# Delta-rule stage: the low parts of the weight chunks move from GpSimd to VectorE

## The chip, the cores and the metric

The kernel runs on one core of a Trainium2 chip. Its time is the device time of that core in microseconds, the median of several executions. The engines are TensorE (PE; PEld is its weight load), VectorE (DVE), ScalarE (ACT), GpSimd (POOL) and SyncE (SP, which issues most of the transfers). The trace comes from one profiled execution.

## The reference, cut to what matters

Two layers work on a sequence of 256 rows and 2048 columns, the first also on a context of 256 rows. The first layer, with the delta rule (a linear recurrence over chunks of 64 rows, 16 heads, both directions), is the one in question:

```python
def _gdn_chunk_scan(q, k, v, g, beta, s0):
    ...
    m = jnp.where(strict, jnp.einsum('bhnid,bhnjd->bhnij', kb, k) * decay, 0.0)
    t_inv = lax.linalg.triangular_solve(eye + m, ..., lower=True, unit_diagonal=True)
    w = jnp.einsum('bhnij,bhnjd->bhnid', t_inv, kb * jnp.exp(gc)[..., None])
    u = jnp.einsum('bhnij,bhnjd->bhnid', t_inv, vb)
    a_intra = jnp.where(tril, jnp.einsum('bhnid,bhnjd->bhnij', q, k) * decay, 0.0)
    def step(S, xs):
        v_new = u_i - w_i @ S
        o = qg_i @ S + a_i @ v_new
        S = S * gl_i[..., None, None] + jnp.swapaxes(kg_i, -1, -2) @ v_new
        return S, o
...
qkv, z_a, ab, b_g, c_g, h_b, z_b = split(h @ w_in)      # projections
y_b = b_g * conv(c_g * h_b, w_conv_b) * silu(z_b)
y   = concat([rmsnorm(o, head_norm) * silu(z_a), y_b]) @ w_out
```

## The kernel before, in words

Every weight passes through `wchunk` (L194 to L214). A chunk of 128 x 1024 floats is loaded by SP into a tile `raw`; ACT rounds it to the format that PE multiplies fastest (`H`, L201); a low part `L` = raw - H is taken either on POOL (L206) or on DVE (L208). The projections then multiply three times per weight tile: H with the high part of the activations, H with their low part, L with their high part (`proj`, L229; `projT`, L238 to L240). There are four buffers each for `raw`, `H` and `L`. Which engine takes the low part is decided by a counter: each chunk adds `LP[stage]`, and when the counter reaches one, POOL takes it and one is subtracted. The stages are 0 (keys and values), 1 (the delta rule), 2 (the first output projection) and 3 (the second layer). Stage 1 has 220 chunks: 32 of wq and 32 of wza, 128 of wbb, and 28 of the output projection.

In stage 1 four groups of four heads are worked off one after the other; I call each a pass. A pass projects its queries (wq) and gate (wza), loads its keys and values from DRAM by POOL's queue (L687), and then runs, in the program's names:

- Gram matmuls `G` and `Q` (L737, L741) and the decay `E` (L746, L748) on PE, exponentials `Es` on ACT, the products `U` and `aT` on DVE (L756, L758);
- a triangular solve of 32 x 32 blocks on DVE: 30 rounds of a product (L778) and an addition (L780) on `LB`, each depending on the one before, with transposes and copies around it, the last ones into `UT` (L797);
- the inverse of the 128 x 128 blocks from these: `PT`, `XT`, `X`, `P` on PE (L806 to L844) with copies between;
- the recurrence, four steps in two directions: `z` (L880), `zk` and `zs` on ACT (L884, L887), `Sp` (L891) and the state `St` on DVE (L896), `kS` (L860), `r` on DVE (L863), `QS` (L868), `az` (L902); at the end the norm, `on` (L916) and the transposes `oT` (L919).

Then come the pass's shares of the projection wbb (3, 4, 5 and 4 blocks of eight chunks) with a short convolution (L930 to L941). Beside all this, `ada_step` loads 256 KB pieces of the modulation weights and accumulates them on DVE (L276).

The order of each engine's instructions is not that of the code: a list scheduler with its own estimate of times puts them in an order, fixed when the kernel is built, with priority for the pass's delta rule (`HP`). So projection chunks of the next pass stand between the solve and the recurrence of this one. Buffers set limits: PSUM has two tiles `pj` for projections and four `g` for everything else in the pass, given out in the code's order; the keys' tile exists once.

Of the kernel before, what the change touches and what calls it, by code (L numbers as in the profile page):

```python
# [29 lines left out]
HP = 1  # L30
FINK = 2
RATE = (2.5, 0.6, 1.2, 0.4)
LP = (0.5, 0.5, 0.4, 0.2)
CHUNKS = (1, 2, 4, 4, 5)
RADII = (1, 2, 4, 8)

# [85 lines left out]
def body(ctx: ExitStack, tc: tile.TileContext, T, dbg=None):  # L122
# [71 lines left out]
    def wchunk(src, nk, rp=None, hp=None, lp=None, sz=1024, HL=None):  # L194
# [7 lines left out]
        L = HL[1] if HL else (lp or wlp).tile([P, sz], F32R, name="L", tag="L")  # L202
        tick[3] += LP[tick[2]]
        if tick[3] >= 1.0:
# [987 lines left out]
```

## Time and profile before

| what | value |
|---|---|
| time, median of 3 runs (lowest to highest) | 2283.49 us (2281.34 to 2284.37) |
| the profiled execution's own time, its span | 2281.2 us, 2279.4 us |
| PE busy | 2102.5 us, 92% of the span |
| DVE busy | 1511.8 us, 66% |
| ACT busy | 992.0 us, 44% |
| POOL busy | 547.9 us, 24% |
| low parts on POOL (L206), on DVE (L208) | 205 at 2483 ns, 349 at 1285 ns in the mean |
| mean granted TensorE clock | 0.968 |

The shares are means over stages with different limits. Stage 1, from the first pass's G to the last pass's oT, lasts from 550 to 1453 us; what bounds it has to be read from that stretch and from its parts. A matmul's duration in the trace is longer than its distance to the next one, since matmuls are pipelined.

### The profile page before, as it was taken

Reading aid. Unit: us, or ns where it says so; the run is one execution under the profiler, and the core shown is the slowest. Engines: PE = TensorE matmul, PEld = TensorE weight load, DVE = VectorE, ACT = ScalarE, POOL = GpSimd, SP = SyncE. Lnnn points to the kernel's source line nnn. Section 1 sums busy time; section 2 is a strip of 40 time slices with the busy share of each in tenths; the row PEclk is TensorE's granted clock in tenths of the full one; section 3 lists DMA queues with packets and bytes.
Section 4 is the critical chain, followed back from the end, with each engine's and each line's share of the span. In section 5 each row is a group of like instructions: output and inputs, shape, how many; then the busy total and the mean of one; then the engine's idle time right before and its main releaser. Section 6 shows DMA issues by size and latency. Waiting matters only on the chain. (4 is left out here: it accounts for less than half of the span.)

```text
span 2279.4 us, 42114 instructions
## 1 busy us (share of the span) xinstructions
PE 2102.5 (92%) x17034; PEld 1951.4 (86%) x17034; DVE 1511.8 (66%) x2500; ACT 992.0 (44%) x1726; POOL 547.9 (24%) x258
## 2 busy tenths in 40 slices
PE   6998999899989988998899879898999999999998
PEld 4888989898979987998899868686789999999886
DVE  4336997658965896599658964666667676555445
ACT  4332354225544635553545354334444444444443
POOL 0112112123322332323232323232112111111221
PEclk9999999999989999999899989999999999999999
DMA  8776546668435663566356645686767656666664
GB/s 324 278 258 209 153 146 201 192 188 275 141 108 169 213 219 122 170 204 214 120 163 214 205 141 175 200 289 193 251 203 215 180 185 199 188 193 216 192 191 137
DMA packets 151267, 446.41 MB, mean 196 GB/s; under 512 B 16512, under 2 KB 23456, under 8 KB 150048
## 3 DMA queue, kind: packets, MB, share of 16 engines
q1 hardware_dynamic: 145936, 425.37, 58.7%
q0 software_dynamic: 5136, 18.35, 2.6%
q8 instruction: 133, 2.18, 0.4%
q14 instruction: 62, 0.51, 0.1%
HBM read 423.19 MB, written 20.46 MB: 195 GB/s over the span
## 5 line engine op out<-in xcount | busy, mean ns | idle before, releaser
L206 POOL TENSOR_TENSOR L<-raw,H 128x1024 fp32r<-128x1024 f32 (+1 forms) x205 | 508.7, 2483 | 1557.9 <-ACT H L201 1500.2
L201 ACT CAST H<-raw 128x1024 fp32r<-128x1024 f32 (+1 forms) x554 | 571.9, 1039 | 698.7 <-PE pj L229 302.3
L208 DVE TENSOR_TENSOR L<-raw,H 128x1024 fp32r<-128x1024 f32 (+1 forms) x349 | 447.8, 1285 | 311.2 <-ACT H L201 310.1
L229 PE MATMUL pj<-hxH,L 128*128 128x256 f32 x1856 | 537.7, 290 | 43.9 <-DVE L L208 43.7
L229 PE MATMUL pj<-hxH,H 128*128 128x256 f32 x1856 | 536.1, 289 | 4.8 <-DVE kacc L482 4.8
L229 PE MATMUL pj<-hxL,H 128*128 128x256 f32 x1856 | 535.0, 288 | 0.0
L229 PEld LDWEIGHTS pj<-hxH,L 128*128 128x128 f32 x1856 | 360.2, 194 | 51.6 <-DVE L L208 48.1
L229 PEld LDWEIGHTS pj<-hxH,H 128*128 128x128 f32 x1856 | 360.2, 194 | 6.9 <-DVE kacc L482 5.0
L229 PEld LDWEIGHTS pj<-hxL,H 128*128 128x128 f32 x1856 | 360.3, 194 | 1.4 <-issue 0.4
L276 DVE SCALAR_TENSOR_TENSOR acc<-araw,cs,acc 128x512 f32<-128x512 f32 x240 | 244.9, 1020 | 134.3 <-DMA araw<-in_ada 84.0
L229 PE MATMUL pj<-h1H,H 128*128 128x256 f32 x1024 | 290.6, 284 | 0.8 <-DVE yo L1052 0.8
L229 PE MATMUL pj<-h1H,L 128*128 128x256 f32 x1024 | 289.8, 283 | 0.0
L229 PE MATMUL pj<-h1L,H 128*128 128x256 f32 x1024 | 289.8, 283 | 0.0
L229 PEld LDWEIGHTS pj<-h1H,H 128*128 128x128 f32 x1024 | 196.5, 192 | 1.1 <-PE adc L286 0.8
L229 PEld LDWEIGHTS pj<-h1L,H 128*128 128x128 f32 x1024 | 196.5, 192 | 0.0
L229 PEld LDWEIGHTS pj<-h1H,L 128*128 128x128 f32 x1024 | 196.5, 192 | 0.0
L229 PE MATMUL pj<-hcH,H 128*128 128x256 f32 x320 | 92.0, 287 | 0.0
L229 PE MATMUL pj<-hcH,L 128*128 128x256 f32 x320 | 91.6, 286 | 0.0
L229 PE MATMUL pj<-hcL,H 128*128 128x256 f32 x320 | 91.5, 286 | 0.0
L238 PE MATMUL pj<-H,y1H 128*128 128x512 f32 x192 | 76.0, 396 | 0.0
L240 PE MATMUL pj<-H,y1L 128*128 128x512 f32 x192 | 75.9, 396 | 0.0
L239 PE MATMUL pj<-L,y1H 128*128 128x512 f32 x192 | 75.9, 395 | 0.0
(433 smaller groups left out, 3852.3 us busy)
## 6 DMA issues: line engine op xcount, KB each, us to landing
raw<-in_wbb SPq DMA_DIRECT2D x128, 512.0 KB, 4.1
raw<-in_wout SPq DMA_DIRECT2D x128, 512.0 KB, 4.5
araw<-in_ada SPq DMA_DIRECT2D x192, 256.0 KB, 3.4
raw<-in_ada SPq DMA_DIRECT2D x64, 512.0 KB, 6.4
raw<-in_wpz SPq DMA_DIRECT2D x64, 512.0 KB, 4.1
raw<-in_wuz SPq DMA_DIRECT2D x64, 512.0 KB, 3.9
raw<-in_wkv SPq DMA_DIRECT2D x40, 512.0 KB, 4.7
araw<-in_ada0g SPq DMA_DIRECT2D x64, 256.0 KB, 3.6
```

The source lines that it names most:

```text
L201: S.copy(H, raw)
L206: G.tensor_tensor(L, raw, H, ALU.subtract)
L208: V.tensor_tensor(L, raw, H, ALU.subtract)
L229: PE.matmul(o[:, e * 256:(e + 1) * 256] if m > 1 else o, w, a[t][:, k, :], start=st and i == 0 and e == 0, stop=sp and i == 2, skip_group_ ...
L238: PE.matmul(o, xH[:, t], H[:, kk, :], start=st, stop=False, skip_group_check=True)
L239: PE.matmul(o, xH[:, t], L[:, kk, :], start=False, stop=False, skip_group_check=True)
L240: PE.matmul(o, xL[:, t], H[:, kk, :], start=False, stop=sp, skip_group_check=True)
L276: V.scalar_tensor_tensor(aacc[u // KT], raw, cs[:, k, 0:1], aacc[u // KT], ALU.mult, ALU.add)
```

## The change

One number of the table `LP` changes, that of stage 1: no chunk there reaches the threshold, so `wchunk` takes its low part on DVE. The other stages keep their shares.

```diff
 RATE = (2.5, 0.6, 1.2, 0.4)
-LP = (0.5, 0.5, 0.4, 0.2)
+LP = (0.5, 0.0, 0.4, 0.2)
```

The scheduler makes a new order from it. On POOL, from the loads of the first pass's keys and values (`KTt`, `Kt`, `Vn`) to the load of the first layer's result (`yld`), only the loads are left:

```order
-L206 TENSOR_TENSOR L<-raw,H 128x1024 x19
+L206 TENSOR_TENSOR L<-raw,H 128x1024 x18
 L687 DMA KTt<-ktd 128x4x512
 L687 DMA Kt<-kkd 128x4x512
 L687 DMA Vn<-vvd 128x4x512
-L206 TENSOR_TENSOR L<-raw,H 128x1024 x26
 L687 DMA Kt<-kkd 128x4x512
-L206 TENSOR_TENSOR L<-raw,H 128x1024
```

110 low parts leave POOL in all. On DVE, in the middle of the second pass's solve (`ltmp` and `LB` are its product and its sum), there stood before:

```order
L778 TENSOR_TENSOR ltmp<-LB 128x234
L208 TENSOR_TENSOR L<-raw,H 128x1024
L276 SCALAR_TENSOR_TENSOR acc<-araw,cs,acc 128x512
L780 TENSOR_TENSOR LB<-LB,ltmp 128x18x13
L778 TENSOR_TENSOR ltmp<-LB 128x238
L931 TENSOR_TENSOR cg<-cg,pj 128x256
L276 SCALAR_TENSOR_TENSOR acc<-araw,cs,acc 128x512
L780 TENSOR_TENSOR LB<-LB,ltmp 128x17x14
L350 SCALAR_TENSOR_TENSOR cbt<-cg,cols,cbt 128x4x63
L778 TENSOR_TENSOR ltmp<-LB 128x240
L351 SCALAR_TENSOR_TENSOR cbt<-cg,cols,cbt 128x4x63
L208 TENSOR_TENSOR L<-raw,H 128x1024
```

and now, from the same round on, with the next pass's query convolution (`ct`, `QT`) between:

```order
L778 TENSOR_TENSOR ltmp<-LB 128x234
L780 TENSOR_TENSOR LB<-LB,ltmp 128x18x13
L208 TENSOR_TENSOR L<-raw,H 128x1024
L778 TENSOR_TENSOR ltmp<-LB 128x238
L362 SCALAR_TENSOR_TENSOR QT<-cth,ct 128x256
L350 SCALAR_TENSOR_TENSOR ct<-pj,conv_124,ct 128x4x63
L780 TENSOR_TENSOR LB<-LB,ltmp 128x17x14
L351 SCALAR_TENSOR_TENSOR ct<-pj,conv_124,ct 128x4x63
L208 TENSOR_TENSOR L<-raw,H 128x1024
L778 TENSOR_TENSOR ltmp<-LB 128x240
```

A low part stands in nearly every round instead of in every second or third; over this whole solve there are 26 low parts where there were 8. On PE, near the end of the second pass's recurrence, projection matmuls (L229) stood between all steps before:

```order
L902 MATMUL az<-zs,aT 128x128 x4
L860 MATMUL kS<-St,KTt 128x128 x4
L868 MATMUL QS<-St,QT 128x128 x4
L229 MATMUL pj<-hxL,H 128x256
L229 MATMUL pj<-hxH,L 128x256
L229 MATMUL pj<-hxH,H 128x256
...
L880 MATMUL z<-r,U 128x128
L229 MATMUL pj<-hxH,H 128x256
L880 MATMUL z<-r,U 128x128 x2
```

and now the steps follow each other without any:

```order
L880 MATMUL z<-r,U 128x128 x4
L891 MATMUL Sp<-zk,Kt 128x128 x4
L902 MATMUL az<-zs,aT 128x128 x4
L860 MATMUL kS<-St,KTt 128x128 x4
L868 MATMUL QS<-St,QT 128x128 x4
L880 MATMUL z<-r,U 128x128 x4
L902 MATMUL az<-zs,aT 128x128 x4
L860 MATMUL kS<-St,KTt 128x128 x4
L868 MATMUL QS<-St,QT 128x128 x4
L880 MATMUL z<-r,U 128x128 x4
L902 MATMUL az<-zs,aT 128x128 x4
L919 MATMUL oT<-cst,on 128x128 x8
```

The projections that stood here are now ahead of this pass's PT, among the chunks of the longer solve. The third and the fourth pass lose theirs in the same way in their last steps, and the fourth also between PT and z.

## Rows read from the trace of the kernel before

**Rows 1.** The table by stretches of stage 1: microseconds from the span's start, length, then busy time (and instructions) of PE, PEld, DVE, ACT and POOL, the granted TensorE clock, the share of the transfer engines and GB/s. For each of the four passes one line from the first G to the first PT, and one from the first z to the first oT.

```profile
550.10:649.10 99.00, 86.22 (x695) 82.98 (x694) 89.73 (x166) 54.77 (x112) 32.87 (x13) 0.98 0.47 150
...
672.20:752.40 80.20, 78.77 (x677) 78.22 (x675) 45.95 (x94) 39.84 (x86) 26.18 (x13) 1.00 0.50 160
757.80:874.90 117.10, 100.64 (x810) 97.77 (x811) 109.02 (x197) 56.15 (x113) 38.83 (x15) 0.98 0.65 209
...
899.00:974.90 75.90, 75.90 (x659) 75.90 (x658) 38.86 (x87) 38.90 (x83) 23.57 (x12) 1.00 0.52 161
979.20:1105.20 126.00, 106.82 (x830) 104.38 (x827) 118.05 (x205) 58.71 (x116) 36.18 (x15) 0.93 0.62 197
...
1129.50:1204.80 75.30, 75.30 (x654) 75.30 (x653) 39.22 (x88) 38.05 (x84) 23.59 (x12) 1.00 0.51 160
1209.50:1334.10 124.60, 101.08 (x749) 96.69 (x748) 116.00 (x204) 61.75 (x120) 34.99 (x14) 0.92 0.62 198
...
1358.70:1453.40 94.70, 87.48 (x491) 75.00 (x490) 41.22 (x83) 42.76 (x82) 24.76 (x11) 0.98 0.55 171
```

**Rows 2.** PE's waits from 550 to 1460 us: what waited, for whom, microseconds in all, how often, the longest.

```profile
PE pj L229 <- DVE L L208: 43.7, 20, 7.4
PE PT L806 <- DVE UT L797: 10.3, 3, 5.3
```

**Rows 3.** POOL in order of time in the second pass's solve: start, duration, instruction, and in brackets the idle time before it with what ended it.

```profile
819.32 2.42 POOL L206 TENSOR_TENSOR L<-raw,H 128x1024 fp32r<-128x1024 f32 x1 [0.57 <-ACT H L201]
```

**Rows 4.** DVE in order of time in the same place, same columns.

```profile
819.40 0.41 DVE L939 SCALAR_TENSOR_TENSOR zb<-zb,pj 128x256 f32<-128x256 f32 x1
819.74 2.16 DVE L778 TENSOR_TENSOR ltmp<-LB 128x130 f32<-128x130 f32 x1
821.82 0.74 DVE L276 SCALAR_TENSOR_TENSOR acc<-araw,cs,acc 128x512 f32<-128x512 f32 x1
...
822.81 0.28 DVE L780 TENSOR_TENSOR LB<-LB,ltmp 128x130 f32<-128x130 f32 x1
823.13 0.32 DVE L778 TENSOR_TENSOR ltmp<-LB 128x150 f32<-128x150 f32 x1
823.36 1.22 DVE L208 TENSOR_TENSOR L<-raw,H 128x1024 fp32r<-128x1024 f32 x1
824.50 0.31 DVE L780 TENSOR_TENSOR LB<-LB,ltmp 128x150 f32<-128x150 f32 x1
```

**Rows 5.** DVE's groups by line in the four stretches from G to PT, the first pass first: count, busy microseconds in all, mean nanoseconds, idle time before them. The first pass's two lines, then the second's four, the third's four and the fourth's four.

```profile
L778 DVE TENSOR_TENSOR ltmp<-LB 128x30 f32<-128x30 f32 (+14 forms) x30 | 19.9, 664 | 0.7
L780 DVE TENSOR_TENSOR LB<-LB,ltmp 128x30 f32<-128x30 f32 (+14 forms) x30 | 12.1, 402 | 0.8
...
L276 DVE SCALAR_TENSOR_TENSOR acc<-araw,cs,acc 128x512 f32<-128x512 f32 x29 | 27.7, 954 | 5.5 <-DMA araw<-in_ada 5.4
L778 DVE TENSOR_TENSOR ltmp<-LB 128x30 f32<-128x30 f32 (+14 forms) x30 | 17.7, 590 | 0.6
L208 DVE TENSOR_TENSOR L<-raw,H 128x1024 fp32r<-128x1024 f32 x14 | 17.0, 1217 | 0.0
L780 DVE TENSOR_TENSOR LB<-LB,ltmp 128x30 f32<-128x30 f32 (+14 forms) x30 | 14.2, 472 | 0.6
...
L276 DVE SCALAR_TENSOR_TENSOR acc<-araw,cs,acc 128x512 f32<-128x512 f32 x30 | 36.5, 1217 | 5.5 <-DMA araw<-in_ada 5.3
L208 DVE TENSOR_TENSOR L<-raw,H 128x1024 fp32r<-128x1024 f32 x15 | 22.6, 1507 | 0.5 <-ACT H L201 0.5
L778 DVE TENSOR_TENSOR ltmp<-LB 128x30 f32<-128x30 f32 (+14 forms) x30 | 15.9, 530 | 0.6
L780 DVE TENSOR_TENSOR LB<-LB,ltmp 128x30 f32<-128x30 f32 (+14 forms) x30 | 9.8, 328 | 0.5
...
L276 DVE SCALAR_TENSOR_TENSOR acc<-araw,cs,acc 128x512 f32<-128x512 f32 x29 | 31.9, 1101 | 5.1 <-DMA araw<-in_ada 5.0
L208 DVE TENSOR_TENSOR L<-raw,H 128x1024 fp32r<-128x1024 f32 x14 | 21.5, 1533 | 0.0
L780 DVE TENSOR_TENSOR LB<-LB,ltmp 128x30 f32<-128x30 f32 (+14 forms) x30 | 14.3, 476 | 0.6
L778 DVE TENSOR_TENSOR ltmp<-LB 128x30 f32<-128x30 f32 (+14 forms) x30 | 9.9, 329 | 0.7
```

**Rows 6.** All engines in order of time in one step of the fourth pass's recurrence (a set of four matmuls has eight records).

```profile
1410.84 1.06 PE L902 MATMUL az<-zs,aT 128*128 128x128 f32 x8
...
1411.74 1.06 PE L860 MATMUL kS<-St,KTt 128*128 128x128 f32 x8
...
1412.83 1.13 DVE L863 SCALAR_TENSOR_TENSOR r<-kS,eg,Vn 128x128 f32<-128x128 f32 x4
...
1417.25 1.05 PE L880 MATMUL z<-r,U 128*128 128x128 f32 x8
...
1418.34 1.14 ACT L884 ACTIVATE zk<-z,nzs 128x128 f32<-128x128 f32 x4 [0.77 <-PE z L880]
```

**Rows 7.** All engines in order of time at the end of the fourth pass.

```profile
1443.97 1.05 PE L880 MATMUL z<-r,U 128*128 128x128 f32 x8
...
1445.70 1.16 PE L902 MATMUL az<-zs,aT 128*128 128x128 f32 x8 [0.68 <-ACT zs L887]
...
1453.42 1.94 PE L919 MATMUL oT<-cst,on 128*128 128x128 f32 x8 [6.56 <-DVE on L916]
```

## The prediction

> **What bounds the kernel now.** I first cut the stage that the change touches into four passes, one for each group of heads, and each pass into stretches by TensorE's own milestones: from the first Gram matmul (G) to the first matmul of the block inverse (PT), from there to the first z, and from the first z to the first oT. The table by stretches [rows 1] then shows two opposite regimes. From G to PT VectorE (DVE) is busy 89.7 of 99.0, 109.0 of 117.1, 118.1 of 126.0 and 116.0 of 124.6 us, while TensorE (PE) is idle for 13 to 24 us in each. From z to oT it is the reverse: PE has no idle time in the second and third pass (75.9 of 75.9, 75.3 of 75.3) and DVE is half idle. GpSimd (POOL) is busy at most 39 us anywhere and limits nothing itself.
>
> The waits of PE over the whole stage [rows 2] say the same: 43.7 us until a low part of DVE (L208), 10.3 us until the last copy of UT on DVE. No wait for a low part of POOL is among them. So from G to PT the end is set by DVE, and what matters is what DVE does there.
>
> POOL matters through DVE. In the second solve POOL's low part runs from 819.32 to 821.74 [rows 3]; DVE's product of 128x130, started at 819.74, ends with it, after 2.16 us, where its neighbour of the same size took 0.28 us, and the one of 150 columns 0.32 us [rows 4]. DVE operations that read one operand from PSUM are not held (L939, 0.41 us at 819.40). The Trainium skill, "SBUF — State Buffer", section "Who interferes with whom", says that a VectorE instruction with two SBUF inputs and a GpSimd instruction that reads SBUF exclude each other, the later one waiting out the whole earlier one; the pair of rows agrees.
>
> **The price of this holding** comes from groups of equal work. The 60 solve operations of a pass take 9.9 + 9.8 = 19.7 us where nothing holds them (the shortest of the four rows of each line); they took 32.0, 31.9, 25.7 and 24.2 us, so 12.3, 12.2, 6.0 and 4.5 us were holding [rows 5]. The 29 or 30 accumulations, 0.744 us each when free [rows 4], lost 6.1, 14.2 and 10.3 us in passes two to four, and DVE's own low parts, 1.22 us when free (the second pass), 4.3 and 4.4 us in the last two [rows 5]. Sums: 12.3, 18.3, 24.5 and 19.2, together 74 us for the 57 low parts that POOL ran there [rows 1], 1.3 us each.
>
> **The change, term by term.** 110 low parts go to DVE. POOL's order loses them all between the loads of K and V. One costs DVE 1.14 us from start to start (823.36 to 824.50 [rows 4]) and takes away 1.3 us of holding: nearly a trade of one for one, were the order unchanged. It isn't. With less of DVE left for it, each solve now stands among more chunks: from a pass's first U to its last UT there are 30, 41, 40 and 31 low parts where there were 12, 15, 14 and 12, and from G to PT PE runs 814, 1035, 1018 and 768 projection matmuls where there were 620, 739, 754 and 700 (counted in units of 256 columns; an out-projection counts two).
>
> From G to PT, DVE: old length, less holding, plus the new low parts at 1.14 us, and about 5 us (estimate: twelve operations of some 0.4 us) for the next pass's query convolution that now stands in the second and third solve. 99.0 - 12.3 + 20.5 = 107; 117.1 - 18.3 + 29.6 + 5 = 133; 126.0 - 24.5 + 29.6 + 5 = 136; 124.6 - 19.2 + 21.7 = 127. PE over the same: a matmul of 256 columns is 0.117 us, since the second z-to-oT stretch of 75.9 us [rows 1] holds 433 of them and 28 sets of four recurrence matmuls at 0.9 us (1410.84 to 1411.74 [rows 6]). With 9 us for G, Q and E that makes 104, 130, 128 and 99 us. DVE remains the longer one, by little except in the last. I add 1 us to each for two engines that wait in turn: 508 us instead of 466.7, **+41**.
>
> From z to oT the pulled-forward matmuls are missing: 438, 78, 252 and 288 units now, 451, 433, 428 and 532 before. That takes 1.5, 41.5, 20.6 and 28.5 us of PE's work out. But they covered the latency of the recurrence, and that cover is gone for most of the second pass, the last two steps of the third and the last four of the fourth. What is laid bare is in [rows 6]: zk ends 2.2 us after z starts, of which PE fills 0.9, so 1.3 idle; without zk, az can start 1.7 us after z [rows 7], 0.8 idle; r ends 2.2 us after kS starts, 0.45 idle where QS stands between and 1.3 where it doesn't. Second pass: four times 1.3 (the first half covered), two of 0.8 and 3.1 for r make 9.5; then az to oT, 7.7 us [rows 7] of which az is 0.9, so 6.8, and 2.5 for the lower clock behind such a pause (eight oT records took 1.94 us there, eight z records 1.05 [rows 7]). Change: -41.5 + 18.8 = -23. Third: 2.5 of step waits, the same tail: -9. Fourth, whose tail was bare already: 5.3: -23. First: -1.5. Together **-56**.
>
> Small terms: PT to z, 41 units more in three passes (+5), and in the last 92 units less with about half of it idle instead (-6): **-1**. From oT to the next G: some matmuls less, a wait for PSUM instead: **+1**. 48 units now stand ahead of the first G: **+6**. Unchanged: casts, transfers, the later stages (220 halves leave the same remainder in the counter of low parts).
>
> Sum: 41 - 56 - 1 + 1 + 6 = **-9 us**. The profiled execution took 2281.2 us, 2.3 below the median of 2283.5; 2283.5 - 9 = 2274.5, so I say **2275**.
>
> **Bounds.** Small groups that the rows leave out were held as well; if another 10 us goes there the sum is -19. If each low part costs DVE its whole 1.22 us, 89 of them add 7 us: -2. The recurrence can cost nothing extra for the clock (-5, -14 in all) or much (below).
>
> **Rivals.** *Slower: the bare recurrence at the lower clock.* Its place is the end of passes two, three and four. PE's work there without cover is some 21, 5 and 14 us; at 1.2 instead of 2.4 GHz these 40 us become 80. It overturns the gain once more than 22% of that work runs low; at half, +20, 2295; at all of it 2315. For it: the granted clock is 0.93 and 0.92 in the stretches where PE idles 19 and 24 us, and 1.00 where it doesn't [rows 1], and the oT records doubled. Against it: each bare wait is 0.45 to 1.3 us, not 6.6. The Trainium skill, "TensorE: Matmul & The Clock Gate", section "Part 1: The HAM clock gate (the "warmup" mystery)", says that an idle array falls to 1.2 GHz until it has been busy for a while; the oT records agree, and by that rule this rival is the one to fear. Chance 0.32.
>
> *No change.* From G to PT, DVE and PE are within 8 us of each other in three passes, and each low part must wait for a cast whose buffers PE frees. If the turns cost 3 or 4 us a pass instead of 1, all is given back: about 2284. For it: 41 us is the difference of large sums. Against it: four buffers of each kind lie between. Chance 0.20.
>
> *Much faster.* POOL's low parts held DVE longer than my rows show. Then DVE falls below PE from G to PT, except in the last pass, and the lengths are PE's, 104, 130 and 128, and some 112 (127 less a quarter of the 63 us below), 34 us less than 508: 2241 to 2250. By the skill's rule as an upper bound, 57 low parts of 2.4 us could hold 137 us; the rows have 74. That the remaining DVE busy time fits the free durations speaks against it. Chance 0.08.
>
> **Chances and range.** Forecast 0.40. A measurement here tells about 0.2%, 4.6 us, from nothing. Faster: forecast and much faster, 0.48; same 0.20; slower 0.32. The forecast's own range is 2264 to 2279. For 8 in 10 the range leaves out the far half of *much faster* and the last part of *slower*: 2252 to 2302.
>
> **What will show it.** Right: PE's waits for L208 fall from 43.7 to under 20 us, and those for UT to near none; the solve operations take about 20 us in every pass; the G-to-PT stretches last about 109, 135, 137 and 127 us and z-to-oT about 79, 53, 66 and 72; no low part of POOL runs between the loads of K and V. Wrong: new PE waits for zk, r or zs above 25 us in all, or a granted clock under 0.9 from z to oT (slower); L208 waits still at 40 us (no change). A wrong order of the two sums, DVE shorter than PE in the last pass, would break the forecast from the other side.

## The result, and the profile after

The changed kernel takes 2244.95 us (median of 4 runs, 2244.31 to 2248.57) against 2283.93 for the kernel before in the same rounds (2281.34 to 2291.99): a ratio of 0.9839, 95% interval 0.982 to 0.9859. Forecast were 2275 us and a range of 2252 to 2302: the sign is right, the gain (39 us for 9) is more than four times the one forecast, and the time lies below the range.

The profiled execution of the changed kernel took 2248.57 us, the slowest of the four; its span is 2246.3, 33.1 us less than before's 2279.4. What follows explains these 33 us; the other 6 of the medians' 39 are between the profiled executions and the medians, and no trace shows them.

| part of the span, us | before | after | forecast of the change | measured |
|---|---|---|---|---|
| start to the first G | 550.1 | 560.8 | +6 | +10.7 |
| G to PT, four passes | 99.0, 117.2, 126.0, 124.6 | 107.8, 132.7, 132.4, 126.2 | +41 | +32.3 |
| PT to z | 23.1, 24.1, 24.3, 24.5 | 23.2, 25.2, 22.3, 16.8 | -1 | -8.5 |
| z to oT | 80.2, 76.0, 75.4, 94.8 | 76.6, 47.5, 63.6, 70.6 | -56 | -68.0 |
| oT to the next G, three | 5.3, 4.2, 4.7 | 5.2, 3.7, 3.7 | +1 | -1.6 |
| behind the last oT | 826.0 | 828.1 | 0 | +2.1 |
| sum | 2279.4 | 2246.3 | -9 | -33 |

The table by stretches of the changed kernel answers to [rows 1]. Columns: start and end, length, busy time of PE, PEld, DVE, ACT and POOL with the number of instructions, granted TensorE clock, share of the transfer engines, GB/s. The stretches are G to PT, PT to z and z to oT of the four passes.

```profile
560.80:668.60 107.80, 107.80 (x891) 105.75 (x890) 93.99 (x191) 63.29 (x120) 0.00 (x0) 1.00 0.55 166
668.60:691.80 23.20, 19.19 (x518) 17.83 (x519) 16.78 (x27) 15.22 (x25) 0.00 (x0) 0.85 0.43 136
691.80:768.40 76.60, 76.60 (x665) 76.60 (x664) 43.32 (x90) 36.33 (x76) 2.25 (x3) 1.00 0.51 159
773.60:906.30 132.70, 132.70 (x1108) 131.49 (x1108) 123.60 (x237) 75.66 (x137) 0.00 (x0) 1.00 0.73 229
906.30:931.50 25.20, 21.35 (x532) 20.19 (x531) 14.29 (x20) 12.00 (x17) 0.00 (x0) 0.86 0.39 124
931.50:979.00 47.50, 37.31 (x303) 35.52 (x302) 25.24 (x75) 20.06 (x60) 2.26 (x3) 0.94 0.39 122
982.70:1115.10 132.40, 131.93 (x1093) 130.83 (x1093) 122.25 (x239) 74.69 (x137) 0.00 (x0) 1.00 0.72 224
1115.10:1137.40 22.30, 19.54 (x523) 18.16 (x523) 13.27 (x17) 12.18 (x16) 0.00 (x0) 0.92 0.42 140
1137.40:1201.00 63.60, 55.37 (x477) 54.83 (x477) 35.93 (x86) 27.90 (x69) 2.25 (x3) 0.98 0.48 150
1204.70:1330.90 126.20, 103.67 (x650) 92.17 (x650) 110.99 (x217) 61.89 (x117) 0.75 (x1) 0.93 0.68 217
1330.90:1347.70 16.80, 11.92 (x449) 11.18 (x449) 7.25 (x12) 8.94 (x14) 0.00 (x0) 0.57 0.23 66
1347.70:1418.30 70.60, 60.98 (x369) 52.79 (x370) 36.29 (x81) 30.55 (x70) 0.00 (x0) 0.97 0.43 138
```

In the first three passes the engine that fills G to PT has changed: PE is busy 107.80 of 107.80, 132.70 of 132.70 and 131.93 of 132.40 us, and DVE now has 9 to 14 us idle. Only in the fourth is DVE still the longer one, with PE idle for 22 us. POOL has no low part left here; the three instructions in some rows are the loads. PE's waits over the stage (560 to 1424 us), answering to [rows 2], say the same:

```profile
PE PT L806 <- DVE UT L797: 19.9, 6, 16.7
PE oT L919 <- DVE on L916: 19.7, 3, 6.6
...
PE az L902 <- ACT zs L887: 4.6, 6, 0.9
...
PE Sp L891 <- ACT zk L884: 2.7, 5, 0.6
...
PE pj L229 <- DVE L L208: 0.8, 1, 0.8
...
PE z L880 <- DVE r L863: 0.5, 1, 0.5
```

The wait of projections for a low part is all but gone: 43.7 to 0.8 us at L229, with another 1.5 us at the output projection's L239, where it was 0.7. The longest wait for UT, 16.7 us, is that of the fourth pass. The bare recurrence shows up as three waits of 6.6 us at the ends of passes two to four, and only 4.6 + 2.7 + 0.5 = 7.8 us for its steps.

DVE's groups by line from G to PT of the second pass (count, busy us, mean ns, idle before) answer to [rows 5]:

```profile
L208 DVE TENSOR_TENSOR L<-raw,H 128x1024 fp32r<-128x1024 f32 x41 | 50.1, 1223 | 0.8 <-ACT H L201 0.7
L276 DVE SCALAR_TENSOR_TENSOR acc<-araw,cs,acc 128x512 f32<-128x512 f32 x29 | 21.8, 752 | 7.2 <-DMA araw<-in_ada 7.2
...
L780 DVE TENSOR_TENSOR LB<-LB,ltmp 128x30 f32<-128x30 f32 (+14 forms) x30 | 9.9, 330 | 0.4
L778 DVE TENSOR_TENSOR ltmp<-LB 128x30 f32<-128x30 f32 (+14 forms) x30 | 9.9, 330 | 0.3
```

In the mean a solve operation takes its free time now (9.9 + 9.9 us for the 60; 17.7 + 14.2 before), an accumulation 0.75 us (0.954 before), a low part 1.22.

Last, one bare step of the second pass, in order of time. It answers to [rows 6]; the step starts at one z and ends at the next, and the last line is the first oT, behind the end of the pass.

```profile
959.00 1.06 PE L880 MATMUL z<-r,U 128*128 128x128 f32 x8
...
960.21 1.16 ACT L884 ACTIVATE zk<-z,nzs 128x128 f32<-128x128 f32 x4
...
960.65 1.27 PE L891 MATMUL Sp<-zk,Kt 128*128 128x128 f32 x8 [0.60 <-ACT zk L884]
961.22 0.64 ACT L887 COPY zs<-z 128x512 f32<-128x512 f32 x1
...
961.90 1.16 PE L902 MATMUL az<-zs,aT 128*128 128x128 f32 x8
...
962.90 1.06 PE L860 MATMUL kS<-St,KTt 128*128 128x128 f32 x8
...
963.79 1.06 PE L868 MATMUL QS<-St,QT 128*128 128x128 f32 x8
963.99 1.13 DVE L863 SCALAR_TENSOR_TENSOR r<-kS,eg,Vn 128x128 f32<-128x128 f32 x4
...
964.68 1.06 PE L880 MATMUL z<-r,U 128*128 128x128 f32 x8
...
978.77 1.94 PE L919 MATMUL oT<-cst,on 128*128 128x128 f32 x8 [6.57 <-DVE on L916]
```

Each set works on four heads, and the next set starts when the first head is ready, not when the set before has ended: Sp starts 0.44 us after zk's first instruction, z starts 0.69 us after r's first (r itself ends at 965.12). The z of 964.68 follows the QS of 963.79 by 0.89 us, a set's own length: there is no wait for r at all. The whole step takes 5.68 us, five sets of 0.9 us and about 1.2 us of waiting and start-up.

### The profile page after: what moved, and what is told of

Read it like the earlier page. It is cut to its first block, busy times and chain, and to the rows that moved or that the text cites. A ratio compares the mean times of both kernels' runs of the same rounds, so it can differ in the third digit from the quotient of the medians.

```text
span 2246.3 us, 42158 instructions
## 1 busy us (share of the span) xinstructions
PE 2093.7 (93%) x17034; PEld 1943.4 (87%) x17034; DVE 1504.6 (67%) x2610; ACT 998.1 (44%) x1726; POOL 269.2 (12%) x148
## 5 line engine op out<-in xcount | busy, mean ns | idle before, releaser
L208 DVE TENSOR_TENSOR L<-raw,H 128x1024 fp32r<-128x1024 f32 (+1 forms) x459 | 565.1, 1234 | 338.4 <-ACT H L201 336.4
L229 PE MATMUL pj<-hxH,H 128*128 128x256 f32 x1856 | 527.5, 284 | 4.8 <-DVE kacc L482 4.4
L229 PE MATMUL pj<-hxH,L 128*128 128x256 f32 x1856 | 528.7, 285 | 3.3 <-DVE L L208 2.8
L229 PE MATMUL pj<-hxL,H 128*128 128x256 f32 x1856 | 528.4, 285 | 0.0
L229 PEld LDWEIGHTS pj<-hxH,H 128*128 128x128 f32 x1856 | 353.5, 190 | 7.0 <-DVE kacc L482 4.6
L229 PEld LDWEIGHTS pj<-hxH,L 128*128 128x128 f32 x1856 | 353.8, 191 | 6.0 <-DVE L L208 3.2
L229 PEld LDWEIGHTS pj<-hxL,H 128*128 128x128 f32 x1856 | 353.8, 191 | 1.5 <-issue 0.4
L206 POOL TENSOR_TENSOR L<-raw,H 128x1024 fp32r<-128x1024 f32 (+1 forms) x95 | 229.8, 2421 | 1030.3 <-ACT H L201 832.3
L276 DVE SCALAR_TENSOR_TENSOR acc<-araw,cs,acc 128x512 f32<-128x512 f32 x240 | 202.3, 843 | 146.0 <-DMA araw<-in_ada 94.9
L229 PE MATMUL pj<-h1H,H 128*128 128x256 f32 x1024 | 291.1, 284 | 0.8 <-DVE yo L1052 0.8
L229 PE MATMUL pj<-h1L,H 128*128 128x256 f32 x1024 | 290.3, 283 | 0.0
L229 PE MATMUL pj<-h1H,L 128*128 128x256 f32 x1024 | 290.2, 283 | 0.0
L229 PEld LDWEIGHTS pj<-h1H,H 128*128 128x128 f32 x1024 | 197.0, 192 | 1.1 <-PE adc L286 0.8
L229 PEld LDWEIGHTS pj<-h1L,H 128*128 128x128 f32 x1024 | 197.1, 192 | 0.0
L229 PEld LDWEIGHTS pj<-h1H,L 128*128 128x128 f32 x1024 | 196.9, 192 | 0.0
L229 PE MATMUL pj<-hcH,L 128*128 128x256 f32 x320 | 91.9, 287 | 0.0
L229 PE MATMUL pj<-hcL,H 128*128 128x256 f32 x320 | 91.8, 287 | 0.0
L229 PE MATMUL pj<-hcH,H 128*128 128x256 f32 x320 | 91.8, 287 | 0.0
```

Source lines behind the costliest of these rows:

```text
L206: G.tensor_tensor(L, raw, H, ALU.subtract)
L208: V.tensor_tensor(L, raw, H, ALU.subtract)
L229: PE.matmul(o[:, e * 256:(e + 1) * 256] if m > 1 else o, w, a[t][:, k, :], start=st and i == 0 and e == 0, stop=sp and i == 2, skip_group_ ...
L276: V.scalar_tensor_tensor(aacc[u // KT], raw, cs[:, k, 0:1], aacc[u // KT], ALU.mult, ALU.add)
```

## The experiments

Two theories stand against each other. **A, holding:** a low part on POOL reads SBUF and holds DVE for more than the 1.14 us which the same low part costs on DVE; with the holding gone, G to PT is set by PE, and the bare recurrence is cheap. **B:** the gain comes from the new order alone, the projections put into other places; how long DVE's operations take matters little. The price of the bare recurrence, on which the rival "slower" rested, is a third question.

In all that follows the kernel before ran on the same chip in the same rounds (2281.5 us in the first four, 2279.2 in the second four), and "stage" is the time from the first G to the last oT, 903.3 us before and 857.5 after.

### POOL writes instead of reading

```diff
-            G.tensor_tensor(L, raw, H, ALU.subtract)
+            G.tensor_tensor(L, raw, H, ALU.subtract) if tick[2] != 1 else G.memset(L.bitcast(F32), 0.0)
```

This is the kernel before (`LP[1]` = 0.5, its order), with POOL's low parts of the delta-rule stage set to zero: the computation leaves out these low parts.

> The kernel before, but in the delta-rule stage GpSimd's half of the low parts are filled with zeros instead of being computed: GpSimd writes, and reads nothing. The low parts of those chunks are left out of the result. The order on every engine has the milestones of the kernel before (projection units from G to PT 594, 740, 752, 701; from z to oT 450, 433, 428, 528). Theory A (GpSimd's reads hold VectorE, and the stretches from G to PT are VectorE's): the solve operations take 20 us in each pass, the four stretches fall from 467 us to about 395, the rest stays; some 2210 us. Theory B (the new order of the changed kernel brought the gain, whoever computes the low parts): about 2280 us, as before.

Measured: 2220.22 us (2213.88 to 2221.3), ratio 0.9728 (0.9706 to 0.975); stage 835.2. The four stretches from G to PT:

```profile
556.50:638.20 81.70, 81.70 (x670) 79.64 (x670) 68.57 (x162) 51.93 (x106) 11.46 (x12) 1.00 0.53 169
744.10:846.20 102.10, 97.98 (x814) 96.68 (x813) 88.25 (x197) 56.48 (x113) 14.36 (x15) 1.00 0.72 239
950.80:1059.80 109.00, 101.86 (x828) 100.09 (x824) 90.70 (x202) 59.05 (x115) 14.72 (x15) 0.98 0.69 226
1162.30:1275.20 112.90, 96.92 (x753) 92.59 (x756) 95.44 (x205) 62.55 (x120) 13.86 (x15) 0.94 0.65 216
```

DVE carries out nearly the same instructions as before (766 in the four stretches, 772 in [rows 1]), and is busy 68.57 + 88.25 + 90.70 + 95.44 = 343.0 us where [rows 1] have 432.8. The six missing instructions account for some 3 us of the difference of 89.8 us; the other 87 us, 1.5 us for each of 57 low parts, are the holding. The same place in the second solve as in [rows 4], in order of time:

```profile
799.25 0.95 POOL L206 MEMSET L<- 128x1024 f32 x1 [4.74 <-PE pj L229]
799.75 0.26 DVE L780 TENSOR_TENSOR LB<-LB,ltmp 128x108 f32<-128x108 f32 x1
...
800.26 0.29 DVE L778 TENSOR_TENSOR ltmp<-LB 128x130 f32<-128x130 f32 x1
```

An addition with both operands in SBUF runs within the memset and takes 0.26 us. In the whole trace the 240 solve operations take 79.1 us, 113.7 before, and 79.1 also in the changed kernel, where POOL has no low part beside them: the memset holds nothing. So it is POOL's reading that holds, and A stands, if 10 us short of its figure for the time. The order alone (B) can't be it: it hardly changed here (594 units instead of 620 in the first G to PT, 740, 752 and 701 instead of 739, 754 and 700 in the others).

### The reading alone, put back

```diff
+            dum.append(tick[2]); (tick[2] == 1 and dum.count(1) < 130 and dum.count(1) % 2 and G.tensor_tensor(yo.rearrange("p a b -> p (a b)"), raw, H, ALU.subtract))
```

The changed kernel; behind DVE's low part, POOL computes that of every second of the first 130 chunks once more, into a tile that nobody reads, 65 in all.

> The changed kernel, with VectorE computing all low parts of the stage, and GpSimd computing every second one once more, in the first three passes, into a tile that nobody reads then (65 operations). The order keeps the changed kernel's shape in these passes (units from G to PT 748, 1034, 994). Theory A: at 1.3 us of holding each, two thirds of them in the stretches from G to PT where VectorE is the longer one, 45 to 75 us slower than the changed kernel: 2290 to 2320. Theory B: GpSimd's spare work costs nothing, about 2245.

Measured: 2310.75 us (2303.5 to 2320.16), ratio 1.012 (1.0091 to 1.0149), 66 us above the changed kernel; stage 923.0. The first two stretches from G to PT, and two of DVE's groups in the second:

```profile
565.90:690.20 124.30, 105.04 (x824) 100.78 (x823) 120.08 (x191) 64.51 (x123) 41.45 (x16) 0.95 0.45 142
801.30:966.50 165.20, 140.07 (x1101) 136.09 (x1100) 161.90 (x235) 74.46 (x136) 58.18 (x21) 0.97 0.59 188
```

```profile
L276 DVE SCALAR_TENSOR_TENSOR acc<-araw,cs,acc 128x512 f32<-128x512 f32 x29 | 31.3, 1079 | 2.1 <-DMA araw<-in_ada 2.1
L778 DVE TENSOR_TENSOR ltmp<-LB 128x30 f32<-128x30 f32 (+14 forms) x30 | 22.7, 756 | 0.3
```

The number of DVE's instructions is that of the changed kernel (191, and 235 against 237), and they take 26 us longer with 16 reads and 38 us longer with 21: 1.6 and 1.8 us a read. Work whose result nobody reads, on an engine with time to spare, costs 66 us. DVE is the engine that fills these two stretches again, busy 120.08 of 124.30 and 161.90 of 165.20 us. One other effect is in the trace: the queue that loads the weight chunks waited 14 times, some 2.2 us each and 31.2 us in all, for a buffer that the repeated subtraction still read. What that adds to the 66 us isn't shown; it doesn't touch the durations of DVE's operations, on which the price of a read rests.

### Half of the change

```diff
-LP = (0.5, 0.0, 0.4, 0.2)
+LP = (0.5, 0.25, 0.4, 0.2)
```

> The share of the delta-rule stage is 0.25: 55 low parts stay on GpSimd. The recurrences of the second and third pass keep their projections (430 and 429 units). Theory A: half the holding is left, 37 of 74 us; with the cover of two recurrences kept, some 2255 to 2270. Theory B: the order in these passes is nearer to the kernel before, 2270 to 2284.

Measured: 2259.26 us (2252.21 to 2265.31), ratio 0.9904 (0.9876 to 0.9931); stage 874.8, solve operations 102.9 us in all, waits for L208 16.7. The recurrence of the second and third pass is still covered in its order (75.6 and 75.8 us from z to oT), and more than half of the gain is there all the same: as expected by A.

### No low part on POOL in any stage

```diff
-LP = (0.5, 0.0, 0.4, 0.2)
+LP = (0.0, 0.0, 0.0, 0.0)
```

> No low part on GpSimd in any stage; the order in the delta-rule stage is that of the changed kernel (units 814, 1035, 1018, 768 from G to PT). Theory A: holding only costs where VectorE is the longer one, which the other stages are not: 2238 to 2250, as the changed kernel. If holding always costs, the 98 further low parts give back 60 us or more: under 2200.

Measured: 2208.44 us (2203.53 to 2211.76), ratio 0.968 (0.9658 to 0.9703). This lies between the two figures, 30 us under A's and 8 us above the other's: I had taken the other stages for untouched by DVE's speed, and the opposite theory gave them too much. The first G comes at 540.0 instead of 560.8, from the last oT to the second layer's first transposes (L1012) it takes 110.2 instead of 121.8 us, behind them 699.4 instead of 706.3; the delta-rule stage hardly differs, 855.1. All accumulations in the trace, the changed kernel first, then this one; and PE's longest waits for the keys' and values' convolution ahead of the first G, in the same order:

```profile
L276 DVE SCALAR_TENSOR_TENSOR acc<-araw,cs,acc 128x512 f32<-128x512 f32 x240 | 202.3, 843 | 146.0 <-DMA araw<-in_ada 94.9 <-DMA araw<-in_ada0g 49.5
```

```profile
L276 DVE SCALAR_TENSOR_TENSOR acc<-araw,cs,acc 128x512 f32<-128x512 f32 x240 | 179.7, 749 | 118.5 <-DMA araw<-in_ada 74.4 <-DMA araw<-in_ada0g 42.7
```

```profile
PE kvp L598 <- DVE kvT L362: 21.1, 8, 4.8
```

```profile
PE kvp L598 <- DVE kvT L362: 9.9, 7, 4.1
```

The accumulations come down to their free 0.749 us everywhere, and PE waits 11 us less for DVE in the first stage. Up to the first G, the changed kernel first, then this one:

```profile
0.00:560.70 560.70, 507.57 (x4317) 472.35 (x4317) 358.68 (x657) 210.15 (x414) 85.06 (x43) 0.97 0.68 222
```

```profile
0.00:540.00 540.00, 502.83 (x4317) 468.99 (x4317) 355.61 (x692) 211.65 (x414) 2.63 (x7) 0.98 0.69 230
```

DVE carries out 35 instructions more here and is busy 3 us less: each of POOL's 36 low parts had held it for 1.2 to 1.3 us (an estimate, with 1.22 us for one on DVE). Behind the last oT, DVE is busy 511.7 us instead of 491.8, with 61 low parts more: about 0.9 us each. So the holding is there in the other stages too, but it is hardly more, or even less, than the low part costs on DVE, and DVE has no less to do. What falls is mostly PE's idle time, from 53.1 to 37.2 us up to the first G. How that divides among DVE's shorter operations, low parts that come earlier and the changed order isn't shown.

### The other stages alone

```diff
-LP = (0.5, 0.0, 0.4, 0.2)
+LP = (0.0, 0.5, 0.0, 0.0)
```

> LP = (0, 0.5, 0, 0): the delta-rule stage keeps the shares of the kernel before, the other three stages give all low parts to VectorE. Theory A (a low part on GpSimd costs VectorE in holding about what it costs on VectorE itself, in every stage; the effects of the stages add): the run without any low part on GpSimd was 36.5 us under the changed kernel, so this one is that much under the kernel before, 2240 to 2250, with the delta-rule stage as before (G to PT 99, 117, 126, 125 us) and the first G some 10 to 20 us earlier than before plus six. Theory B (the gain of the run without any came from the delta-rule stage, whose neighbours no longer hand over GpSimd work at its edges): within 10 us of before, 2273 to 2291.

Measured: 2247.34 us (2241.52 to 2253.16), ratio 0.9852 (0.9828 to 0.9876), within A's figures; B's lower end is 26 us above. From G to PT 93.8, 117.8, 125.0 and 123.2 us, near the kernel before, where I had expected its 99 also in the first pass. The first G came 8.3 us earlier than before, not 10 to 20. The sizes add: this edit saves 1.5% of the time, that of the case 1.6%, both together 3.2%.

### The price of the bare recurrence

```diff
-            rs = B.tile([P, 256], F32, name="rs", tag="qs")
+            rs = I.tile([P, 256], F32, name="rs", tag="ltmp")
```

The changed kernel with one small tile in another buffer. It was held up by the short convolution of the pass before; freed of that, the scheduler puts other projections beside the recurrences, as the expectation tells.

> The changed kernel with rs in another buffer (L708, the product's tile instead of the one shared with the short convolution), which lets the order keep projections beside the recurrence of the second and third pass (459 and 578 units from z to oT instead of 78 and 252) and leaves none for the solve of the fourth (0 instead of 768); the first three solves keep their chunks (814, 1034, 1029). Theory A (bare steps are cheap: what the second pass's recurrence loses to waits is 47.5 - 78 x 0.117 - 25.2 = 13 us): z to oT of the second pass 79 us, of the third 93, so these two grow by about 61 us, while the fourth solve, alone on VectorE, gets shorter by only 27 low parts, about 31 us, with PE idle there: 20 to 35 us slower than the changed kernel, 2265 to 2280. The slower rival (bare steps are dear, covering them pays): the two stretches grow by under 40 us, and the time is 2245 or less.

Measured: 2262.65 us (2261.45 to 2264.01), ratio 0.9928 (0.9902 to 0.9953); stage 877.5, 20.0 us more than the changed kernel: the lower edge of A, whose figure for the time itself begins 2 us higher. From z to oT of the second and third pass, and G to PT of the fourth:

```profile
921.90:1000.90 79.00, 79.00 (x685) 79.00 (x685) 45.88 (x98) 37.15 (x79) 2.25 (x3) 1.00 0.53 170
1162.20:1257.20 95.00, 93.50 (x624) 84.72 (x623) 53.71 (x104) 43.65 (x86) 2.99 (x4) 1.00 0.53 175
1262.60:1342.90 80.30, 15.83 (x72) 11.79 (x73) 70.87 (x169) 27.86 (x79) 0.00 (x0) 0.58 0.46 142
```

The second pass's recurrence got 381 units of projection more (459 for 78), 44.6 us of PE's work, and is only 31.5 us longer: 13.1 us is what it costs bare, of which 6.6 is its end. The projections are better kept for the fourth solve, which here leaves PE with 15.83 us of work in 80.3. (That solve got 46 us shorter, where A said 31: DVE is busy 40.1 us less, 33 of them for 27 low parts, and idle 5.8 us less.) The rival that feared the bare recurrence is refuted: its stretches would have grown by under 40 us, and they grew by 62.9.

### Fewer accumulations in the stage

```diff
-RATE = (2.5, 0.6, 1.2, 0.4)
+RATE = (2.5, 0.4, 1.2, 0.4)
```

> The changed kernel with RATE of the delta-rule stage 0.4 instead of 0.6: a third fewer accumulations (L276) on VectorE per chunk there, the rest later. The solves are shorter for it in the order: 814, 861, 803, 768 units from G to PT, and 438, 261, 440, 288 from z to oT. Theory A (VectorE sets G to PT; each accumulation and low part counts): G to PT of the second pass 112 to 118 us, of the third 108 to 114, the sum of the eight stretches falls by about 10 us, the later stages pay some 5 us for the accumulations: 2235 to 2245. Theory B (PE sets G to PT in the first three passes, VectorE is covered): the eight stretches sum to what they do in the changed kernel, 2245 to 2252.

Measured: 2241.69 us (2238.39 to 2250.21), ratio 0.9839 (0.9812 to 0.9867), that of the changed kernel: as a time it falls into A's figures, but it tells no gain. From G to PT and z to oT of the second and third pass, and G to PT of the fourth:

```profile
773.70:886.30 112.60, 112.60 (x930) 111.75 (x929) 104.80 (x213) 67.29 (x128) 0.00 (x0) 1.00 0.66 202
910.20:974.80 64.60, 56.38 (x487) 55.83 (x486) 36.20 (x86) 28.82 (x70) 2.25 (x3) 0.98 0.46 147
978.10:1082.90 104.80, 104.80 (x877) 103.97 (x873) 97.78 (x202) 60.86 (x118) 0.00 (x0) 1.00 0.65 198
1106.50:1183.20 76.70, 76.70 (x666) 76.70 (x665) 43.20 (x89) 36.49 (x76) 2.25 (x3) 1.00 0.50 159
1187.80:1314.20 126.40, 102.90 (x645) 91.28 (x645) 111.93 (x218) 63.45 (x121) 0.75 (x1) 0.92 0.67 220
```

PE is busy all the time in the second and third solve, and these got shorter by what was taken out of them: 174 and 215 units at 0.117 us are 20 and 25 us, measured 20 and 28. That alone doesn't decide, since DVE's busy time fell by nearly as much (18.8 and 24.5 us). What decides is that PE has no idle time in these stretches and DVE has 7 to 8 us: PE sets these lengths, as B says. The fourth, with the same projections and the same 29 accumulations as in the changed kernel, stays at 126.4. B's sum, however, was wrong: the eight stretches fell by 17 us (757 to 740), not by none, because the projections cover more of two recurrences, whose bare cost falls from 13 to about 9 and from 9 to 0 us. In the profiled execution, which is 8.5 us above the median, the stage gains 15.7 us and the part behind the last oT loses 17.0; the next edit, set against the version without any low part on POOL, shows 14.2 and 19.7. What the stage gains by postponing accumulations is lost behind it.

### Both

```diff
-LP = (0.5, 0.0, 0.4, 0.2)
+LP = (0.0, 0.0, 0.0, 0.0)
-RATE = (2.5, 0.6, 1.2, 0.4)
+RATE = (2.5, 0.4, 1.2, 0.4)
```

> No low part on GpSimd anywhere and RATE of the delta-rule stage 0.4. If both edits add: the run without any low part (2208) plus what the rate alone does to the changed kernel (theory A -5, theory B 0 to +5): 2203 by A, 2208 to 2213 by B.

Measured: 2211.41 us (2209.7 to 2213.85), ratio 0.9702 (0.968 to 0.9723): B. It can't be told from the version without the second edit (0.968). That one, no low part on POOL at all, is the fastest full kernel of the study, at 2208.44 us.

## Why the prediction was wrong in size, point by point

**The holding: right in kind, too small.** The solve operations were to fall by 12.3 + 12.2 + 6.0 + 4.5 = 35 us and fell by 34.6; the waits for L208 were to fall under 20 us and fell to 0.8. But the sum over all operations, 74 us from [rows 1, 5], is about 87 by the experiment in which POOL only writes. I had given what the rows leave out 10 us as a bound; it is some 13. A low part thus costs DVE 1.14 us and gives back 1.5, not 1.3. The forecast called this "nearly a trade of one for one"; at 1.5 us for 1.14 it is a gain.

**G to PT, +41 forecast, +32.3 measured: the step "DVE remains the longer one, by little" failed.** It took the old lengths, in which DVE had 8 to 9 us idle [rows 1], and added to them; the idle time, in passes two to four mostly for accumulation data that had not landed [rows 5], was counted as DVE's work. DVE's busy time is 94.0, 123.6 and 122.3 us in the first three passes, below PE's work. Their lengths are PE's, forecast as 104, 130 and 128 and measured as 107.8, 132.7 and 132.4 (3 to 4 us more for what the sum left out). The rival "much faster" had this mechanism: DVE below PE in three passes. It gave this stretch 34 us less than 508, and was right on the mechanism and wrong on the last pass, 112 forecast and 126.2 measured. There the forecast's DVE sum, 127 us, came out, in part by luck: DVE is busy 111.0 us and idle 15.2, where the sum held 118.5 and 8.6.

**z to oT, -56 forecast, -68.0 measured: the step that priced the bare recurrence by the ends of whole sets failed.** The second pass was to lose 18.8 us to waits and lost 13.2 (47.5 less 78 units of 0.117 and 25.2). The items of the 18.8 add up to 19.2, since four times 1.3, two of 0.8 and 3.1 make 9.9 and not 9.5. Three of them were too dear. The 3.1 us for r came from r's end, 2.2 us after kS starts [rows 6]; but z needs only r's first head, kS and QS fill the time until then, and the pass loses 0.7 us there, in one place. The 1.3 us for a step with zk came from zk's end in the same way; a bare one costs 1.1 us (in the step shown, z and Sp together take 2.90 us instead of 1.8), and the trace has three of them, not four. The 2.5 us for the lower clock stand behind the first oT (978.77, 1.94 us for eight records, as in [rows 7]), outside the stretch in which I counted them, and those records tell only 0.9 us (1.94 for 1.05). These three items are 6.7 us too much; the two steps without zk and the 6.8 us of the end were about right. The third pass was to lose 2.5 + 6.8 + 2.5 and lost 8.9 (63.6 less 252 units of 0.117 and 25.2), about the first two. PE's wait in the end is 6.6 us, three times. The first pass also gave up 1.4 us of waits that it had before (78.77 busy of 80.20 [rows 1], now 76.60 of 76.60); I had not counted them.

**PT to z, -1 forecast, -8.5 measured.** The 41 units added in the first three passes were to cost 5 us and cost nothing: these stretches were 71.4 us together and are 70.7. In the kernel before:

```profile
649.10:672.20 23.10, 20.77 (x505) 19.43 (x506) 11.50 (x14) 9.31 (x14) 3.15 (x2) 0.73 0.30 96
...
874.90:899.00 24.10, 20.55 (x517) 19.28 (x518) 14.23 (x19) 12.57 (x18) 4.71 (x2) 0.83 0.33 95
...
1105.20:1129.50 24.30, 21.24 (x507) 19.78 (x508) 14.35 (x19) 11.84 (x18) 5.89 (x2) 0.72 0.35 116
```

The added projections did not go into idle time: PE had 8.9 us of it here and has 10.6 now. Its busy time fell from 62.6 to 60.1 us, with some 5 us of projections more in it, and the granted clock rose from 0.73, 0.83 and 0.72 to 0.85, 0.86 and 0.92. The clock is the likely reason, which the forecast left out; no run changes it alone. In the last pass 24.5 became 16.8, -7.7 where I said -6.

**The small terms.** 48 units ahead of the first G are 5.6 us; measured were 10.7. The same 2266 units stand ahead of it in the run with the moved cover, where it came at 553.7, and in that with fewer accumulations, 561.3: single executions differ here by more than the term, and I can't settle it. The oT-to-G stretches got shorter by 1.6 us instead of longer by 1.

**The clock rival did not come.** Its 40 us of bare work at half clock would have shown as a granted clock well below 0.9 from z to oT; it is 1.00, 0.94, 0.98 and 0.97. What is lacking lies in the pauses at the ends: in the second pass the clock is 1.00 from 931.5 to 972.1 us, 0.59 from there to 979.0, and 0.50, the level of 1.2 GHz, from 979.0 to 982.7. The waits inside bare steps are 0.9 us at most. The Trainium skill, "TensorE: Matmul & The Clock Gate", section "Part 1: The HAM clock gate (the "warmup" mystery)", says that an idle array falls to 1.2 GHz; the trace agrees for the pauses of 6.6 and 16.7 us (0.57 in the stretch behind the latter) and shows no fall for the short ones of the recurrence. Between PT and z, among matmuls of 32x32, it did fall beside short waits too (0.92 in the third pass, whose longest is 1.1 us). At 0.32 this rival's chance was far too high; the argument against it, that the waits are short, was the one to trust.

**No change** needed turns between DVE and PE of 3 or 4 us a pass; PE has no idle time in the first two solves and 0.5 us in the third, so there are none. Of the signs named ahead, the one for UT was wrong: near no wait was forecast, 19.9 us were measured, though the forecast's own sums for the fourth pass, 127 for DVE and 99 for PE, called for a wait there.

Put together: of the 24 us by which the forecast of the span missed, 12 are the recurrence, 9 G to PT, 7.5 PT to z, 2.6 oT to G, and 7 of the start and the end go the other way.

## What to carry to other kernels

An operation that is moved to an idle engine need not be free: here GpSimd's reads of SBUF held VectorE. Compare the free duration of the busy engine's operations with their mean in the stage, sum the excess over all groups, and set it against the price of doing the work at home. When an engine's load in a stretch is summed up, leave out its idle time, put the other engine's sum beside it and take the longer of the two. Price a dependent step by when the first head of each set is ready and what fills the time until then, and check in which stretch a cost falls before it is added there.

## What the runs showed of the hardware

A POOL subtraction of 128x1024, some 2.4 to 2.7 us long, took 1.5 to 1.8 us from DVE in this stage, more than the 1.14 us for which DVE does the subtraction itself. A POOL memset of the same tile, 0.95 us, took nothing from it. The Trainium skill, "SBUF — State Buffer", section "Who interferes with whom", says that a VectorE instruction with two SBUF inputs contends with a GpSimd instruction that reads SBUF, not with one that only writes it; both runs agree with that, and the price comes from them. I had not expected that low parts on POOL cost time in the other stages too, where DVE is far from full (343 us busy in the first 540 of the kernel before): without them there the time falls by another 1.6%, though DVE is busy only 3 us less up to the first G and 20 us more behind the last oT.
